# The MLP's first layer as seven block products with tokens on the partitions

## The chip, the core and the metric

The kernel runs on one core of a Trainium2 chip. A core has a matrix engine (TensorE, PE in the profile; its weight loads are PEld), VectorE (DVE), ScalarE (ACT), GpSimd (POOL) and SyncE (SP), each of which works through its own instructions in order and waits for the others by semaphores. SP, ACT and POOL issue DMAs. The metric is the device time of one execution in microseconds (us), the median of several runs.

## The reference, cut to what matters

One layer of a decoder trunk on 512 tokens of 2048 features, in float32. The mixing part and a cross-attention to 256 memory tokens come first; the change touches the MLP, the last norm, and how the cross-attention's last projection hands its result on.

```
h = h + memory_cross_attention(rmsnorm(h, g_xattn), rmsnorm(mem, g_mem), xa_wq, xa_wkv, xa_wo)
hn = rmsnorm(h, g_mlp)                                  # h: 512 x 2048
h = h + square(relu(hn @ w_ff1)) @ w_ff2                # w_ff1: 2048 x 8192, w_ff2: 8192 x 2048
return rmsnorm(h, g_final)
```

## The kernel before

**Three matmuls for one.** Every operand is split into a high part, rounded to the fast matmul format, and a low part, the rest. A product is hi·hi + hi·lo + lo·hi: three matmuls of 128x512 (L349 to L351 in the helper `mm`; L1490 to L1492 in the second layer). The high part is made by a cast on ACT, the low part by a subtraction on DVE that waits for the cast.

**First layer** (`mlp`, L1269 to L1301). Features lie on the partitions and the 512 tokens on the columns. 64 tiles `f` of 128 hidden features, each 16 blocks of the inner dimension by three matmuls into one PSUM bank (`ft`). `Stream` loads the weights on SP's queue, splits them three units ahead (L356 on ACT, L357 on DVE). `evac1` (L1275 to L1279) does relu and the norm's factor on DVE, the square on ACT, and ACT sends the tile to DRAM (`d_u`). After tiles 7, 15, 23 and 31 `res_T` (L1303) transposes a quarter of the residual to token rows, 16 transposes into four banks, and puts it back into the same SBUF tiles (`rp`, shown as `d`).

**Second layer** (`Second`, L1315). Tokens on the partitions, and a block scheme: activation and weight are cut in halves, and seven products of sums of halves take the place of eight. A *chunk* (eight of them) is one such scheme over 1024 hidden features: seven *products* n = 0 to 6, each of four *steps* `kk`; a step uses one weight block of 128x1024, or a sum of such blocks, and has 12 matmuls. For n = 0, 3 and 5 the block is a plain load on SP's queue; for n = 1, 2, 4 and 6 it is added by an accumulating DMA, issued by POOL, onto the block of an earlier product (L1352), which must wait until that one's low part is made (L1362). So cast (L1357), low part, accumulating DMA, cast of the sum is a chain from product to product. `prep` writes the casts four steps ahead of the matmuls, the low parts three, the loads seven. `stat` and `stat_low` (L1387, L1392) split the activation sums, one product ahead. `use` (L1494) adds or subtracts the four finished banks into the residual on DVE. `ahead` starts all this under the last six tiles of the first layer.

**End** (`Final`, L1502). While the last product runs, tokens 0 to 255 are normed: squares with row sums on ACT, factor, scaling on DVE, transposes back to features, gain during the evacuation, and out by SP. Then tokens 256 to 383 and 384 to 511, the latter wholly after the last matmul.

**Order.** Nothing schedules: each engine runs its instructions as the Python code emits them. PSUM has eight banks: four `mm`, three `st`, one `o`.

Of the kernel before, what the change touches and what calls it, by code (L numbers as in the profile page):

```python
# [72 lines left out]
def _units(a):  # L73
# [49 lines left out]
    feat("f1", a["w_ff1"][0].reshape(KT, 128, DFF), DFF // 128)  # L123
# [8 lines left out]
class _Null:  # L132
# [8 lines left out]
    def __getitem__(self, k):  # L141
        return self
# [21 lines left out]
class Slots:  # L164


    def __init__(self, pool, name, n, cols):
        self.pool, self.name, self.cols = pool, name, cols
        self.free, self.of, self.low = deque(range(n)), {}, n

# [6 lines left out]

    def put(self, t):
        self.free.append(self.of.pop(id(t))[0])


class Stream:
# [4 lines left out]
    def __init__(self, k, dram, order, info):  # L187
# [5 lines left out]
        self.last = len([t for t in order if t[0] != "f2"]) if order else 0  # L193
# [116 lines left out]
class Layer:  # L310
    def __init__(self, tc, ctx, a, order, info):
# [16 lines left out]
        self.d_u = dr.tile([8, 2, 2, 128, 4, 256], F32, name="d_u")  # L328
        self.slots = Slots(sp, "s", N_SLOTS, 1024)
# [874 lines left out]
    def cross(self, rate):  # L1204
# [29 lines left out]
        self.HG = [self.slot_hl() for _ in range(KT)]  # L1234
        self.acc = self.PP[:, 2048:]
        later = deque()
        for f in range(4):
            ps = [self.new_mm() for _ in range(4)]
            for h in range(2):
                w = self.W.get(("xo", f, h))  # L1240
                for kk in range(2):
                    k = 2 * h + kk
                    if f == 0 and k == 3:
                        self.side.drain()
                    for j in range(4):
# [4 lines left out]
                        if later and k < 3:  # L1250
                            self.res_use(later.popleft(), G_MLP, self.HG, st)
# [6 lines left out]
        while later:  # L1258
            self.res_use(later.popleft(), G_MLP, self.HG, st)
        self.put(*self.pt, *ks, *vs, *sl, *ssl, *self.oX)  # L1260

    def res_use(self, d, g, hg, st):
        self.split(hg[d], self.RES[d], self.gains[:, g + d:g + d + 1])
# [3 lines left out]
    def mlp(self, out):  # L1267

        nc = self.nc  # L1269
        tmp, sl = self.halves(2)  # L1270
        us, usl = self.halves(4)

        def evac1(f, ps):
            t, u = tmp[f % 2], us[f % 4]
            nc.vector.scalar_tensor_tensor(t, ps, 0.0, self.rbc, op0=OP.max, op1=OP.mult)  # L1275
            nc.scalar.activation(u, t, AF.Square)  # L1276
            c, h, k = f // 8, f // 4 % 2, f % 4
            nc.scalar.dma_start(self.d_u[c, h, :, :, k, :].rearrange("t p n -> p t n"),
                                u.rearrange("p (t n) -> p t n", t=2))  # L1279

        def on1(k):
            if k == 1:
                self.rx3 = self.col_stats(self.acc, "rx3")
            if k == 6:
                self.bcast(self.rx3, self.rbc)

        ps0 = self.ft("f1", 0, self.HG)
# [334 lines left out]
```

## Time and profile before

| | us |
|---|---|
| median of 3 runs (2961.63 to 2963.34) | 2962.59 |
| the profiled execution | 2963.05 |
| its span in the trace | 2961.0 |
| PE busy / DVE / ACT / POOL | 2909.2 / 1648.9 / 1237.9 / 295.4 |
| first layer: 1603.4 to 2310.1 | 706.7 |
| second layer up to the last product: 2310.1 to 2919.4 | 609.3 |
| last product, last norm and output: 2919.4 to the end | 41.6 |

The engines' busy times overlap, so they don't add up to the span. [...] DVE and ACT rows follow each other closer than their durations too.

### The profile page before, as it was taken

How to read it: one execution, taken by the hardware profiler on the slowest of the kernel's cores; microseconds unless marked ns; L12 is line 12 of the kernel's file. 1: busy time of each engine (PE TensorE's matmuls, PEld its weight loads, DVE VectorE, ACT ScalarE, POOL GpSimd, SP SyncE). 2: the span in 40 equal slices, each digit the busy share in tenths (PEclk: the TensorE clock that was granted, in tenths of full speed). 3: DMA queues.
4: the chain of work that ended last, by engine and by line, in shares of the span. 5: the costliest groups of instructions: out<-in, count | busy, mean ns of one | idle time of the engine just before them, and what ended most of it. 6: DMA issues, size and time to landing. Idle time of an engine off the chain costs nothing.

```text
span 2961.0 us, 38469 instructions
## 1 busy us (share of the span) xinstructions
PE 2909.2 (98%) x14386; PEld 2483.1 (84%) x14386; DVE 1648.9 (56%) x3112; ACT 1237.9 (42%) x2460; POOL 295.4 (10%) x524
## 2 busy tenths in 40 slices
PE   8999999999999999999999999999999999999997
PEld 8999989888888888888887888888888788888885
DVE  6346666655555555554457332322333688888886
ACT  6345555544444444323345322322222444444444
POOL 3110200011001001001103000000000111111110
PEclk9999999999999999999999999999999999999998
DMA  4321212222233346543322334333335788888884
GB/s 154 105 71 57 66 54 65 62 93 93 93 100 97 121 132 201 172 140 119 118 84 89 118 118 121 118 117 121 125 119 166 183 218 218 218 222 217 216 220 123
DMA packets 139067, 387.85 MB, mean 131 GB/s; under 512 B 14208, under 2 KB 37120, under 8 KB 138880
## 3 DMA queue, kind: packets, MB, share of 16 engines
q1 hardware_dynamic: 96128, 288.92, 30.6%
q0 software_dynamic: 18432, 67.12, 11.8%
q10 hardware_dynamic: 24320, 29.37, 2.8%
q8 instruction: 112, 1.84, 0.3%
q14 instruction: 75, 0.61, 0.1%
HBM read 351.79 MB, written 33.55 MB: 130 GB/s over the span
## 4 chain that ended last, share of the span: by engine, by line
PE 88%; DVE 4%; ACT 3%; issue 3%; DMA 2%; POOL 0%; SPq 0%; ACTq 0%; POOLq 0%; DVEq 0%
PE mm L349 21%; PE mm L351 21%; PE mm L350 21%; PE mm L1492 3%; PE mm L1490 3%; PE mm L1491 3%; PE st L570 2%; PE st L1492 2%; PE st L1491 2%; PE st L1490 2%; DMA s<-wts 2%; DVE s L357 1%; PE o L587 1%; PE o L588 1%; PE st L351 1%
## 5 line engine op out<-in xcount | busy, mean ns | idle before, releaser
L349 PE MATMUL mm<-s,s 128*128 128x512 f32 (+5 forms) x3032 | 1152.3, 380 | 7.2 <-ACT s L356 5.4
L351 PE MATMUL mm<-s,s 128*128 128x512 f32 (+5 forms) x3032 | 1128.1, 372 | 2.8 <-DVE s L360 2.8
L350 PE MATMUL mm<-s,s 128*128 128x512 f32 (+5 forms) x3032 | 1127.2, 372 | 0.2 <-DVE s L357 0.2
L357 DVE TENSOR_TENSOR s<-s,s 128x512 fp32r<-128x512 f32 (+4 forms) x814 | 533.8, 683 | 445.9 <-ACT s L356 442.4
L349 PEld LDWEIGHTS mm<-s,s 128*128 128x128 f32 x3032 | 572.1, 189 | 96.5 <-issue 8.0
L351 PEld LDWEIGHTS mm<-s,s 128*128 128x128 f32 x3032 | 570.7, 188 | 92.7 <-DVE s L360 4.8
L350 PEld LDWEIGHTS mm<-s,s 128*128 128x128 f32 x3032 | 572.5, 189 | 81.6 <-DVE s L357 1.3
L356 ACT CAST s<-s 128x512 fp32r<-128x512 f32 (+4 forms) x814 | 451.7, 586 | 313.4 <-PE mm L350 156.7
L1357 ACT CAST s<-s 128x1024 fp32r<-128x1024 f32 x224 | 227.3, 1049 | 273.2 <-DMA s<-wts 262.9
L1362 DVE TENSOR_TENSOR s<-s,s 128x1024 fp32r<-128x1024 f32 x224 | 269.9, 1222 | 77.1 <-ACT s L1357 76.0
L497 ACT ACTIVATE PP<-PP,mx 128x512 f32<-128x512 f32 (+1 forms) x208 | 116.3, 559 | 274.6 <-DVE mx L496 273.9
L1352 POOL DMA_DIRECT2D s<-wts x128 | 111.5, 871 | 1179.2 <-DVE s L1362 1037.7
L357 DVE TENSOR_TENSOR s<-st,s 128x512 fp32r<-128x512 f32 (+5 forms) x265 | 140.6, 540 | 111.6 <-ACT s L356 110.6
L1492 PE MATMUL mm<-s,s 128*128 128x512 f32 x512 | 200.3, 391 | 1.7 <-DVE s L1392 1.4
L1491 PE MATMUL mm<-s,s 128*128 128x512 f32 x512 | 199.9, 390 | 1.7 <-DVE s L1362 1.7
L1490 PE MATMUL mm<-s,s 128*128 128x512 f32 x512 | 200.6, 392 | 0.0
L1275 DVE SCALAR_TENSOR_TENSOR s<-mm,rbc 128x512 f32<-128x512 f32 x64 | 44.3, 692 | 276.9 <-PE mm L351 276.9
L1276 ACT ACTIVATE s<-s 128x512 f32<-128x512 f32 x64 | 40.4, 632 | 365.3 <-DVE s L1275 365.3
L356 ACT CAST s<-st 128x512 fp32r<-128x512 f32 (+5 forms) x265 | 117.4, 458 | 49.0 <-PE st L447 29.3
L496 DVE CUSTOM_DVE_ANT_0 PP<-st,cst 128x512 f32<-128x512 f32 (+1 forms) x208 | 99.9, 481 | 45.9 <-PE st L351 45.2
L1492 PEld LDWEIGHTS mm<-s,s 128*128 128x128 f32 x512 | 96.4, 188 | 24.5 <-DVE s L1392 4.5
L1492 PE MATMUL st<-s,s 128*128 128x512 f32 x288 | 112.6, 391 | 3.3 <-DVE s L1392 3.3
(235 smaller groups left out, 3076.7 us busy)
## 6 DMA issues: line engine op xcount, KB each, us to landing
s<-wts SPq DMA_DIRECT2D x388, 512.0 KB, 3.6
s<-wts POOLq DMA_DIRECT2D x128, 512.0 KB, 9.3
s<-wts SPq DMA_DIRECT2D x64, 352.0 KB, 3.0
d_u<-s ACTq DMA_DIRECT2D x64, 256.0 KB, 2.1
s<-d_u SPq DMA_DIRECT2D x32, 512.0 KB, 7.8
d_g<-s ACTq DMA_DIRECT2D x32, 256.0 KB, 2.0
s<-d_g SPq DMA_DIRECT2D x32, 256.0 KB, 4.0
s<-wts SPq DMA_DIRECT2D x16, 384.0 KB, 3.1
```

The lines of the kernel that those rows point to most:

```text
L349: t.matmul(ps, a.hr, b.hr, start=first, stop=False)
L350: t.matmul(ps, a.hr, b.lr, start=False, stop=False)
L351: t.matmul(ps, a.lr, b.hr, start=False, stop=last)
L356: nc.scalar.copy(o.hr, src)
L357: nc.vector.tensor_sub(o.lr, src, o.hi)
L497: nc.scalar.activation(p, p, AF.Exp, bias=mx, scale=-1.0, accum_out=sm)
L1352: self.nc.gpsimd.dma_start(t, src, accum_op=OP.add)
L1357: self.nc.scalar.copy(t.hr, self.raw[i])
L1362: self.nc.vector.tensor_sub(t.lr, r, t.hi)
L1490: m(ps, a.hr, b.hr, start=first, stop=False, skip_group_check=True)
L1491: m(ps, a.hr, b.lr, start=False, stop=False, skip_group_check=True)
L1492: m(ps, a.lr, b.hr, start=False, stop=last, skip_group_check=True)
```

## The change

**First layer in the second layer's manner.** `Mlp` takes the place of `mlp` and `Second`. Each of eight chunks now gives 1024 hidden features for all tokens in seven products over the 2048 inner features: 56 products, again of four steps of 12 matmuls, and then the 56 of the second layer, in one loop. The weight blocks (`f1` repacked on the host) use the same loads, accumulating DMAs, casts and low parts. The activation sums are formed in the first chunk and kept; `stat` splits two halves for each product. `use1` evacuates two banks after every product: copies on ACT for n = 0 to 2, add or subtract, relu and factor on DVE and squares on ACT for n = 3 to 6.

**Turned by transposes.** The result has tokens on the partitions, and the second layer needs features there. `u_T` does it: four transposes into the one `o` bank, a copy on ACT, a DMA to `d_u` issued by ACT; four such jobs after n = 4 and four after n = 6, one at the head of a step.

**Residual through DRAM.** `res_T` becomes 16 jobs in the first 16 steps, each four transposes into `o`, a copy on ACT and a DMA to `d_r`. Its SBUF is lent to weight blocks. Near the end of the first layer `res_in` reads it back, eight DMAs of 512 KB.

**Hand-over.** `res_use` writes the scaled input with two 256-column activations on ACT instead of a 512-column split. The first layer's first loads and splits run in the last quarter of the cross-attention's output projection (`f` = 3).

**End.** `gain_rows` spreads the last gain over the partitions by 16 small matmuls. `square` takes the row sums and multiplies the gain in before the factor is known, for all rows that are complete; the scaling is shared by DVE and ACT, and outputs leave by SP and ACT.

```
-    feat("f1", a["w_ff1"][0].reshape(KT, 128, DFF), DFF // 128)
+    f1 = a["w_ff1"][0].reshape(2, 4, 2, 128, 8, 2, 512)
...
+                        if f == 3 and j == 3:
+                            mlp.ahead(k)
...
-    def res_use(self, d, g, hg, st):
-        self.split(hg[d], self.RES[d], self.gains[:, g + d:g + d + 1])
+    def res_use(self, d, mlp, st):
+        for t in range(2):
+            self.nc.scalar.activation(mlp.x(d, t), self.RES[d][:, 256 * t:256 * t + 256], AF.Copy,
+                                      scale=self.gains[:, G_MLP + d:G_MLP + d + 1])
...
+        last = 2 * self.NP - 1
+        for p in range(last):
+            n, layer = p % 7, p // self.NP
...
+            for j in range(4):
+                i = 4 * p + j
+                self.prep(i + AHEAD)
+                if j == 0:
+                    self.blocks(p + 1)
+                if j % 2 == 0 and j // 2 < nh:
+                    self.stat(p + 1, j // 2)
+                if j % 2 and j // 2 < nh:
+                    self.stat_low(p + 1, j // 2)
+                for _ in range(1 + layer):
+                    if self.jobs and self.jobs[0][0] <= i:
+                        self.jobs.popleft()[1]()
+                self.part(p, j, ps, range(2))
...
+            (self.use2 if layer else self.use1)(p, ps)
+            if p == self.NP - 4:
+                self.res_in()
...
+    def use1(self, p, ps):
...
+            if n < 3:
+                nc.scalar.copy(o, ps[t])
+                continue
...
+            nc.vector.tensor_scalar(o, ps[t] if n == 6 else o, 0.0, r, op0=OP.max, op1=OP.mult)
+            nc.scalar.activation(o, o, AF.Square)
+        if n in (4, 6):
+            b = blk[1] if n == 4 else 0
+            cs = [C.pop((t, b)) for t in range(2)]
+            for j in range(4):
+                self.jobs.append((4 * p + 6, lambda j=j: self.u_T(c, b, j, cs, p == self.NP - 1)))
...
+    def u_T(self, c, b, j, cs, last):
+        k, nc = self.k, self.nc
+        ps, u = k.new_st() if last else k.new_o(), self.half()
+        for t in range(4):
+            o = t % 2 * 512 + j * 128
+            nc.tensor.transpose(ps[:, t * 128:t * 128 + 128], cs[t // 2][:, o:o + 128], k.ident)
+        nc.scalar.copy(u, ps)
+        nc.scalar.dma_start(k.d_u[c, b, :, :, j, :].rearrange("t p n -> p t n"), u.rearrange("p (t n) -> p t n", t=2))
...
+        self.gain_rows(Y)
+        self.prep(4 * p + 3)
+        for t in (0, 1, 2, 3):
+            for q in range(2, 4) if t > 1 else range(4):
+                self.square(t, q)
+        self.scale([0, 1])
+        for j in range(4):
+            self.part(p, j, X, [0])
+        self.use2(p, X, [0])
...
+        for t in range(2):
+            for q in range(4):
+                self.back(t, q, Y[q])
+        self.scale([2])
+        for j in range(4):
+            self.part(p, j, X, [1])
...
+    def square(self, t, q):
+        x = self.row(t, q)
+        self.nc.scalar.activation(self.sq[:, q % 2 * 512:q % 2 * 512 + 512], x, AF.Square,
+                                  accum_out=self.cols[:, 4 * t + q:4 * t + q + 1])
+        self.nc.vector.tensor_mul(x, x, self.g[q // 2][:, q % 2 * 512:q % 2 * 512 + 512])
```

**What stands on ACT in the first layer.** `s` are SBUF tiles, `PP` and `d` SBUF lent or shared, `o` the single PSUM bank. Before, inside the first layer (weight casts of 512 columns, a square and its store for each tile):

```order
L356 CAST s6_93<-s0_87 128x512 x2
L356 CAST s2_89<-s1_88 128x512 x2
L1276 ACTIVATE s11_14117<-s9_14115 128x512
L1278 DMA d_u_86<-s11_14117 128x2x256
L356 CAST s4_91<-s0_87 128x512 x2
L356 CAST s6_93<-s1_88 128x512 x2
```

In the changed kernel, from the third step of a product n = 5 to the second step of n = 6 (L1350 casts a weight block, L1423 an activation sum, L1540 squares, L1578 copies the transposed tile out of `o`, L1579 stores it):

```order
L1350 CAST s37_15345<-d0_10557 128x1024
L1423 CAST s9_15350<-s20_13692 128x1024
L1578 COPY s29_14128<-o_15353 128x512
L1579 DMA d_u_86<-s29_14128 128x2x256
L1350 CAST s21_15372<-PP_100 128x1024
L1578 COPY s15_14129<-o_15378 128x512
L1579 DMA d_u_86<-s15_14129 128x2x256
L1540 ACTIVATE d4_10556<-d4_10556 128x512 x2
L1350 CAST s24_15403<-d3_10555 128x1024
L1423 CAST s16_15408<-s12_13685 128x1024
L1578 COPY s15_14129<-o_15411 128x512
L1579 DMA d_u_86<-s15_14129 128x2x256
```

Each copy that frees the `o` bank now stands behind the casts of weights four steps ahead, and, at a product's start, behind the squares of the product just finished.

**What stands on ACT at the hand-over.** Before, the last four feature tiles (L359 split, L420 square for the norm) and then the weight casts of the first layer:

```order
L359 ACTIVATE s32_13699<-d0_10556,gains_95 128x512
L420 ACTIVATE s36_13683<-d0_10556 128x512
L356 CAST s2_89<-s0_87 128x512 x2
L356 CAST s4_91<-s1_88 128x512 x2
L356 CAST s6_93<-s0_87 128x512
```

In the changed kernel, after the last four feature tiles (the first cast, L1350, takes the first accumulated block; L1567 copies a residual tile out of `o`):

```order
L1350 CAST s17_14132<-PP_100 128x1024
L1423 CAST s33_14140<-s31_14137 128x1024
L1567 COPY s29_14128<-o_14143 128x512
L1568 DMA d_r_87<-s29_14128 128x512
L1350 CAST s39_14162<-PP_100 128x1024
L1567 COPY s15_14129<-o_14168 128x512
L1568 DMA d_r_87<-s15_14129 128x512
```

The first copy out of `o` (tile o_14143, which PE fills at the head of the layer's first step) now stands behind the cast of the first accumulated block.

**What stands on DVE at the end.** Before, from the last additions into the residual (L1497) to the factor of tokens 0 to 255 (L392 to L397):

```order
L1497 TENSOR_TENSOR d2_10553<-st_22613,d2_10553 128x512
L1497 TENSOR_TENSOR d3_10554<-st_22614,d3_10554 128x512
L1497 TENSOR_TENSOR d2_10553<-st_22615,d2_10553 128x512
L1497 TENSOR_TENSOR d3_10554<-o_22616,d3_10554 128x512
L1362 TENSOR_TENSOR s8_22671<-s35_22133,s19_22670 128x1024
L1521 TENSOR_REDUCE PP_99<-PP_99 128x2
```

In the changed kernel, from the last of these additions (L1553):

```order
L1553 TENSOR_TENSOR s27_18978<-o_23593,s27_18978 128x512
L1355 TENSOR_TENSOR s38_23648<-d4_10556,s12_23647 128x1024
L1641 TENSOR_TENSOR d4_10556<-d4_10556,d2_10554 128x512 x2
L1641 TENSOR_TENSOR s31_18977<-s31_18977,d0_10557 128x512 x2
L1641 TENSOR_TENSOR s27_18978<-s27_18978,d2_10554 128x512 x2
L1641 TENSOR_TENSOR s26_18979<-s26_18979,d0_10557 128x512 x2
L1641 TENSOR_TENSOR s37_18981<-s37_18981,d0_10557 128x512 x2
L1641 TENSOR_TENSOR s34_18983<-s34_18983,d0_10557 128x512 x2
L1647 TENSOR_REDUCE PP_100<-PP_100 128x2
```

Twelve multiplications by the gain (L1641), each behind its square on ACT, moved ahead of the first factor.

## Rows read from the trace of the kernel before

**Rows 1.** The page's part 1: busy us, share of the span, instructions.

```profile
PE 2909.2 (98%) x14386; PEld 2483.1 (84%) x14386; DVE 1648.9 (56%) x3112; ACT 1237.9 (42%) x2460; POOL 295.4 (10%) x524
```

**Rows 2.** Stretches: start:end, length, busy by engine, TensorE clock, DMA share, GB/s.

```profile
1603.40:2310.10 706.70, 705.40 (x3153) 585.37 (x3153) 217.86 (x330) 200.14 (x344) 6.18 (x4) 1.00 0.40 124
2310.10:2339.10 29.00, 24.02 (x97) 19.00 (x96) 19.99 (x20) 12.93 (x13) 7.09 (x8) 0.94 0.96 208
2339.10:2919.40 580.30, 578.64 (x2545) 476.98 (x2544) 477.50 (x511) 265.93 (x269) 104.38 (x120) 1.00 0.86 214
2919.40:2961.00 41.60, 21.39 (x113) 17.19 (x111) 22.30 (x65) 19.54 (x57) 0.00 (x0) 0.81 0.34 101
```

**Rows 3.** Timeline of PE (start, us, instruction): 40 matmuls apart; four transposes between matmuls.

```profile
2313.95 0.40 PE L1492 MATMUL mm<-s,s 128*128 128x512 f32 x1
...
2323.03 0.39 PE L1490 MATMUL st<-s,s 128*128 128x512 f32 x1
...
2932.39 0.60 PE L1542 MATMUL st<-cst,d 128*128 128x128 f32 x4
...
2932.75 0.48 PE L1490 MATMUL mm<-s,s 128*128 128x512 f32 x1
...
2933.06 0.39 PE L1491 MATMUL mm<-s,s 128*128 128x512 f32 x1
```

**Rows 4.** Timeline of PE at the second layer's start; in brackets idle time and releaser.

```profile
2312.21 0.50 PE L1491 MATMUL mm<-s,s 128*128 128x512 f32 x1 [1.69 <-DVE s L1362]
...
2326.94 0.50 PE L1492 MATMUL st<-s,s 128*128 128x512 f32 x1 [3.29 <-DVE s L1392]
...
2327.64 0.63 PE L1491 MATMUL st<-s,s 128*128 128x512 f32 x1
...
2330.91 0.40 PE L1490 MATMUL st<-s,s 128*128 128x512 f32 x1
```

**Rows 5.** Timeline of ACT in the first layer: square, store, next cast.

```profile
1807.01 0.63 ACT L1276 ACTIVATE s<-s 128x512 f32<-128x512 f32 x1 [5.77 <-DVE s L1275]
1807.67 0.37 ACTq L1278 DMA_DIRECT2D d_u<-s  x1
1808.13 1.66 ACT L356 CAST s<-s 128x512 fp32r<-128x512 f32 x3 [0.49 <-ACT s L1276]
```

**Rows 6.** The page's part 5: busy, mean ns of one, idle before and releaser.

```profile
L1357 ACT CAST s<-s 128x1024 fp32r<-128x1024 f32 x224 | 227.3, 1049 | 273.2 <-DMA s<-wts 262.9
L1362 DVE TENSOR_TENSOR s<-s,s 128x1024 fp32r<-128x1024 f32 x224 | 269.9, 1222 | 77.1 <-ACT s L1357 76.0
```

**Rows 7.** The accumulating DMAs of line L1352, issue to landing.

```profile
DMA to landing us min/median/max: 5.3/9.3/12.3
```

**Rows 8.** The page's part 6: issues, KB each, median us to landing.

```profile
s<-d_u SPq DMA_DIRECT2D x32, 512.0 KB, 7.8
```

**Rows 9.** Timeline of DVE, ACT and POOL at the hand-over to the first layer.

```profile
1591.47 2.47 DVE L1254 TENSOR_TENSOR d<-mm,d 128x512 f32<-128x512 f32 x4
...
1595.08 0.62 ACT L420 ACTIVATE s<-d 128x512 f32<-128x512 f32 x1
...
1606.01 6.41 POOL L421 TENSOR_TENSOR PP<-PP,s 128x512 f32<-128x512 f32 x4 [3.78 <-ACT s L420]
```

**Rows 10.** Timeline at the end: squares, reduce, scaling, last matmul, last gain.

```profile
2919.04 0.64 ACT L1517 ACTIVATE PP<-d 128x512 f32<-128x512 f32 x1
...
2919.80 0.64 ACT L1517 ACTIVATE PP<-d 128x512 f32<-128x512 f32 x1
...
2924.34 0.16 DVE L1521 TENSOR_REDUCE PP<-PP 128x2 f32<-128x8 f32 x1 [2.91 <-ACT PP L1517]
...
2925.76 3.26 DVE L1527 TENSOR_SCALAR d<-d,rx 128x512 f32<-128x512 f32 x8
...
2941.76 0.39 PE L1492 MATMUL mm<-s,s 128*128 128x512 f32 x1
...
2956.98 0.37 ACT L1550 ACTIVATE s<-o,gains 128x128 f32<-128x128 f32 x1 [0.42 <-DVE s L1552]
```

More of the change, by code (lines that the diff above doesn't have):

```diff
@@ L192, in __init__ @@
         self.log = []
-        self.last = len([t for t in order if t[0] != "f2"]) if order else 0
+        self.last = len([t for t in order if t[0] not in ("f1", "f2")]) if order else 0
     def src(self, tag):
@@ L1468, in run @@
-        fin = Final(k, out)
-        self.prep(4 * last + 3)
-        fin.stats([0, 1])
-        first = fin.steps([0, 1], Y)
-        for t in range(2):
-            for j in range(2):
-                for kk in range(4):
-                    self.mm(ps[2 * t + j], A, kk, t, self.hl[4 * last + kk], j, False, kk == 3)
-                    if t or j:
-                        next(first, None)
-                self.use(ps[2 * t + j], a, b, t, j, sign)
-            if t == 0:
-                fin.stats([2])
@@ new lines, in run, with part @@
+            (self.use2 if layer else self.use1)(p, ps)
+            if p == self.NP - 4:
+                self.res_in()
+        self.end(last, X, Y, out)
+    def part(self, p, j, ps, ts):
+        n = p % 7
+        B = self.hl[4 * p + j]
+        first, last = self.FIRST[n] and j == 0, j == 3
+        for t in ts:
+            if p < self.NP:
+                S = self.S[p, j // 2][0]
+                for i in range(2):
+                    o = (2 * j + i) % 4 * 256 + 128 * t
+                    self.mm(ps[t], S[:, o:o + 128], B[:, 512 * i:512 * i + 512], first and i == 0, last and i == 1)
+            else:
+                S, o = self.S[p, 0][0], 256 * j + 128 * t
+                for i in range(2):
+                    self.mm(ps[2 * t + i], S[:, o:o + 128], B[:, 512 * i:512 * i + 512], first, last)
+        if 1 in ts:
+            self.k.put(B.hi, B.lo)
+            if j == 3 or j == 1 and p < self.NP:
+                self.k.put(S.hi, S.lo)
@@ L1489, in mm @@
+    def mm(self, ps, a, b, first, last):
         m = self.nc.tensor.matmul
@@ new lines, in row, with end @@
+    def row(self, t, q):
+        return self.R[t][q // 2][:, q % 2 * 512:q % 2 * 512 + 512]
+    def end(self, p, X, Y, out):
+        k = self.k
+        self.out = out
+        k.put(*self.usl)
+        self.sq = k.slots.plain()
+        self.cols = k.acc
+        self.gain_rows(Y)
[7 more added lines that the diff above has]
+        self.use2(p, X, [0])
+        self.square(2, 0)
+        self.square(2, 1)
+        for t in range(2):
+            for q in range(4):
+                self.back(t, q, Y[q])
+        self.scale([2])
+        for j in range(4):
+            self.part(p, j, X, [1])
+        self.use2(p, X, [1])
+        self.square(3, 0)
+        self.square(3, 1)
+        for q in range(4):
+            self.back(2, q, Y[q])
+        self.scale([3])
+        for q in range(4):
+            self.back(3, q, X[q])
```

383 lines of the change are left out of this document (198 added, 185 removed).

## The prediction

> **What bounds the kernel.** I read the busy line first: PE 98% [rows 1], so a term counts only where it adds or takes PE time. Then the stretches [rows 2]. The first layer, 706.7 us, is PE throughout, with DVE and ACT under a third busy and the DMA at 0.40. The second layer between its start and its last product is PE too, but with DVE at 82%, ACT at 46% and the DMA at 0.86: that is the surrounding into which the first layer now moves. Two stretches are not PE-bound: the second layer's first 29.0 us and the last 41.6 us. Last I read pitches: 40 matmuls take 2323.03 - 2313.95 = 9.08 us, 0.227 us each [rows 3]. A step of 12 is 2.72 us, a product of 48 is 10.9 us.
>
> **1. Matmuls.** The first layer has 64 x 16 x 3 = 3072 matmuls, afterwards 56 x 48 = 2688. 384 fewer x 0.227 = -87.1 us, all of it on PE's path.
>
> **2. Transposes.** 64 jobs `u_T` of four. A group between matmuls costs 2933.06 - 2932.39 less one pitch, 0.44 us [rows 3]: +28.2 us. The residual's 64 transposes are there before and after. One spreading of the norm's factor over the partitions (four small matmuls, at that group's price twice) goes: -0.9 us.
> The row says that transposes are not paid at their duration: four take 0.60 us together. [...]
>
> **3. Start of the first layer.** The block scheme pays its start-up at the hand-over now. The old hand-over was nearly free: the first stretch has 1.3 us without PE [rows 2]. New chain: the first residual tile of `f` = 2 is ready at 1591.5 + 0.6 = 1592.1 [rows 9]; ACT then writes four tiles, about 1.27 us each (two half activations, estimated at 0.37 from a 512-column one at 0.62, and a square at 0.53), to 1597.3. A cast of the sum and one of the first block, 1.05 each [rows 6], to 1599.4; the low part, 1.22 [rows 6], to 1600.6; the accumulating DMA, 9.3 [rows 7], to 1609.9; its cast, and a cast of the next sum, to 1612.0; only then the copy that frees `o`, 0.6, at 1612.6. PE begins step 0 at 1603.4 and is at step 1's transposes at 1606.6: it waits 6.0 us. [...] POOL's four additions for the norm, 1.6 us each [rows 9], stand before the fourth accumulating DMA, so that it lands near 1623.7 and costs 1 us at product 1; the next ten steps each have a residual job and lose some 3 us in all in the way of term 4. Together 12 us against 1.3: +10.8 us (ends +5 and +18).
>
> **4. The `o` bank in every chunk.** One bank serves all jobs, so the transposes at the head of a step wait for the copy of the step before. That copy stands on ACT behind casts for four steps later. On ACT a job costs 0.59 for the copy and 0.45 until the next cast can start: from the end of the square at 1807.64 to the next cast is 0.49 us, since ACT waits to issue the store [rows 5]. I lay out one chunk with PE at 0.227, casts at 1.0 to 1.05, low parts at 1.22 [rows 6], accumulated blocks landing 9.3 after the low part [rows 7].
> - Product n = 6 begins at 0. ACT must first square the results of n = 5, which DVE finishes only at 1.25; squares end at 1.9. Two casts to 4.0, copy to 4.6. PE wants to transpose at 3.15: it waits 1.5 us.
> - n = 0 begins at 13.25 and its fourth block's low part is made at 15.3, behind the evacuation of n = 6. The sum for n = 1 lands at 24.65, its cast ends at 25.7, the copy behind it at 26.3. PE is there at 25.0: 1.35 us.
> - In n = 1 ACT copies two banks, casts a block and a sum, and copies at 30.45; PE is there at 29.5: 1.0 us.
> - n = 2 to 5 have no such wait in this layout, and low parts are ready 2 us or more before their step.
> 3.85 us a chunk; the first wait eight times, the others seven: 12.0 + 16.5 = +28.5 us. No row shows a short wait of this kind, hence both ends: nothing, since the second layer hardly waits for its weights after its start (2545 x 0.227 = 577.7 of 580.3 us [rows 2]), up to 50 us, if each of the 16 groups loses a whole queue of three casts, 3.1 us. I take the layout, which lies nearest to the durations of the rows.
>
> **5. Second layer.** Its start-up goes: 29.0 us for 96 matmuls, 21.8 us, is 7.2 us lost [rows 2, 4]. In one loop the weights are already running: -6.7 us with half a us left over. Reading back the residual puts 4.2 MB into a stretch where the DMA is 0.86 busy at 214 GB/s [rows 2], for which that rate needs 20 us; a 512 KB read takes 7.8 us there [rows 8]. Accumulated blocks in flight are held up, with 2 us or more of slack: +4 us, ends 0 and +13. The first layer's own DMA moves as much as the second's, at the same pace.
>
> **6. End.** Before: 22.4 us from 2919.4 to the last matmul, 19.2 from there to 2961.0 [rows 2, 10]. After, from the same zero: gain matmuls to 1.8 (16 x 0.11); four copies on ACT to 2.8; twelve squares at a pitch of 0.76 [rows 10], to 11.9, where eight were; the multiplications on DVE end at 12.6, the factor takes 1.42 (reduce to scaling [rows 10]), scaling starts at 14.05. PE has done half of the last product at 7.3 and waits until 14.5. Then 32 transposes; the second four groups need banks that DVE empties only after two additions and two multiplications, at 19.2. The second half of the product starts at 21.5, its last matmul at 26.8, later at the lower clock: 4.4 to 6.6 us late. Behind it, in place of 19.2: addition, square and product to 2.7, copies to 3.9, factor to 5.35, scaling, transposes and copies to 8.4, and 3.7 from the last evacuation to the end [rows 10]: 12.1, so 7.1 won. Net -1.5 us (ends -3 and +5).
>
> **Sum.** -87.1 + 28.2 - 0.9 + 10.8 + 28.5 - 6.7 + 4.0 - 1.5 = -24.7. The profiled execution took 2963.05 us, 2.05 more than its span, which stay. 2963.05 - 24.7 = 2938.3; it stands 0.46 above the median, so I say **2938 us**.
>
> **Rivals.**
> - **The `o` bank never stops PE.** If ACT keeps ahead, term 4 falls to nothing and term 3 to its lower end: 2938 - 28.5 - 5.8 = 2904; with a third of term 4 left, 2914. For it: after its start the second layer loses under 3 us to waits [rows 2]. Against: there no ACT instruction stood between two uses of a bank by PE within one step.
> - **Slower: accumulated blocks land later.** Each chunk has two links from low part to landing, n = 0 to 1 and 1 to 2, whose casts stand before copies that PE waits for. Every us over 9.3 then costs up to 2 us a chunk, 16 us in all. It decides from 1.5 us over, 10.8 us; the slowest landing now is 12.3 [rows 7], which as a median would add 48 us: 2986. Against: the DMA carries no more than in the second layer. 6%.
> - **Transposes at their full duration.** If the groups did not overlap here, each transpose would cost the last one's own 0.60 - 3 x 0.11 = 0.27 us [rows 3]: 256 x 0.16 = 41 us more, 2979. [...] Against: every group in the rows overlaps. 1%.
> - **Start-up and reading back at their upper ends**, +7 and +9, with the end at +5: 2938 + 22.5 = 2960.
> - **The matmuls are not saved.** In the built program's order PE has 3072 fewer of the first layer's matmuls and 2688 more of the second's kind, so this is out: 1%, the time would be 2938 + 87 = 3025.
>
> **Chances.** Forecast with its neighbourhood (2920 to 2950) 0.60; bank free (2900 to 2920) 0.20; upper ends (2950 to 2965) 0.12; later blocks 0.06; full transposes 0.01; matmuls not saved 0.01. The range reaches over the first two and half of the third: 2905 to 2957. A measurement of this kernel tells about 0.2%, 5.9 us, from no change. Faster by more: 0.60 + 0.20 + half of 0.12 and a little, 0.87; within: 0.06; slower: 0.07.
>
> **What would show it.** The first layer should take 683 to 690 us from the first product to the last, with PE's waits put down to ACT's copy out of `o`, some 1 to 1.5 us each, three in a chunk, and one of about 6 us in its first product. The second layer should start without a wait over 1 us. DVE in the first layer near 80% busy, DMA near 0.85. In the end PE should stand still for some 7 us in the middle of the last product, and 12 us should follow the last matmul. The forecast is wrong if PE in the first layer waits for low parts (blocks too late), if the waits at `o` are absent, or if the matmuls' pitch there is not 0.227.

## The result

| | us |
|---|---|
| median of 4 runs before | 2962.75 |
| median of 4 runs after (2923.53 to 2926.27) | 2925.05 |
| ratio after to before, 95% interval | 0.9873 (0.9856 to 0.989) |
| span of the profiled execution, before and after | 2961.0, 2923.1 |

The change wins 37.7 us; the forecast was 24.7 (2938, range 2905 to 2957). The sign and the range held, and the `o` bank does stop PE behind ACT's copies as forecast, but at one of the three places of the forecast's layout; at the layer's start the chain was another one, and several terms were off in size.

First the page's part 1 of the changed kernel (answers [rows 1]) and its stretches, as in [rows 2]: first layer from its first matmul to the second layer's first, second layer up to the last product, and the end.

```profile
PE 2857.5 (98%) x14282; PEld 2438.4 (83%) x14282; DVE 1896.4 (65%) x3224; ACT 1484.4 (51%) x2663; POOL 405.6 (14%) x652
```

```profile
1601.18:2283.14 681.96, 654.31 (x2999) 535.92 (x2998) 475.64 (x463) 438.70 (x535) 120.06 (x133) 0.99 0.85 212
2283.14:2883.36 600.22, 600.22 (x2658) 497.38 (x2656) 495.68 (x527) 277.36 (x281) 108.78 (x125) 1.00 0.88 218
2883.36:2923.10 39.74, 25.44 (x145) 22.34 (x143) 25.93 (x57) 22.64 (x55) 0.00 (x0) 0.89 0.39 106
```

Against [rows 2] the first layer is 24.7 us shorter, the second 9.1 (29.0 + 580.3 before), the end 1.9. The other 2.2 lie ahead of the first layer: its start was at 1600.3 to 1603.8 in the fourteen traces of this study, which have nearly all the work ahead of it in common, so that is scatter. In the first layer PE is busy 654 of 682 us; the second has no gap left. The waits of PE that remain (line that waits, tile, releaser, total us, times, longest), the five largest that stand on lines of the MLP:

```profile
PE o L1577 <- ACT s L1578: 12.5, 12, 1.4
PE o L1566 <- ACT s L1567: 8.7, 2, 7.3
PE o L1577 <- ACT d L1540: 6.4, 1, 6.4
PE st L1661 <- issue: 5.2, 1, 5.2
PE mm L1661 <- DVE s L1656: 3.5, 1, 3.5
```

L1577 is the transposes of `u_T`, L1566 those of `res_T`, L1661 those of the end.

To price terms I laid the trace out by steps: the time from the first matmul of a step to that of the next, less twelve pitches of 0.2268 us (a matmul shows a duration of 0.39 us there, but in a row the next one starts 0.227 us later). Over the 224 steps of the first layer this excess adds up to 72.3 us. "Loss" below is this excess without the transpose groups.

| term, us | forecast | measured |
|---|---|---|
| 1 matmuls | -87.1 | -87.1 (pitch unchanged) |
| 2 `u_T` groups, factor broadcast | +27.3 | +29.8 (64 x 0.48 - 0.9) |
| 3 start of the first layer | +10.8 | +9.4 (10.7 against 1.3) |
| 4 `o` bank in the chunks | +28.5 | +15.3 |
| 5 second layer's start; reading back | -6.7; +4 | -10.5; +9.3 |
| 6 end | -1.5 | -1.9 |
| ahead of the change | 0 | -2.2 |
| sum | -24.7 | -37.9 (as the spans) |

**Term 4 in the trace.** Timeline of the changed kernel at the head of a product n = 6 that begins at 1851.9 (start, us, instruction, in brackets idle time and releaser); first ACT, then the transposes on PE in front of the product's second step:

```profile
1852.99 0.63 ACT L1540 ACTIVATE d<-d 128x512 f32<-128x512 f32 x1 [0.73 <-DVE d L1539]
1853.53 1.03 ACT L1350 CAST s<-PP 128x1024 fp32r<-128x1024 f32 x1
1854.47 1.04 ACT L1423 CAST s<-s 128x1024 fp32r<-128x1024 f32 x1
1855.41 0.58 ACT L1578 COPY s<-o 128x512 f32<-128x512 f32 x1
```

```profile
1856.05 0.66 PE L1577 MATMUL o<-cst,s 128*128 128x128 f32 x4 [1.13 <-ACT s L1578]
```

Square of n = 5's result, two casts, copy: the order of the forecast, at 1.36 us in each of eight chunks by the step table (forecast 1.5). The other two waits of its layout, 1.35 and 1.0 us about the head of n = 1, are not there. In their place four of eight chunks lose 0.6 to 1.7 us in n = 5, which the layout had without a wait.

**Term 3 in the trace.** ACT, POOL and PE at the start of the changed kernel's first layer:

```profile
1606.18 0.63 ACT L442 ACTIVATE s<-d 128x512 f32<-128x512 f32 x1 [2.35 <-POOL PP L443]
...
1608.40 0.63 ACT L442 ACTIVATE s<-d 128x512 f32<-128x512 f32 x1 [0.78 <-POOL PP L443]
1608.93 1.03 ACT L1350 CAST s<-PP 128x1024 fp32r<-128x1024 f32 x1
...
1610.82 0.58 ACT L1567 COPY s<-o 128x512 f32<-128x512 f32 x1
```

```profile
1604.56 8.22 POOL L443 TENSOR_TENSOR PP<-PP,s 128x512 f32<-128x512 f32 x4
1612.73 0.89 POOL L1345 DMA_DIRECT2D s<-wts  x1
```

```profile
1611.44 1.12 PE L1566 MATMUL o<-cst,d 128*128 128x128 f32 x4 [7.27 <-ACT s L1567]
```

The copy ends at 1611.4 (forecast 1612.6) but not for the forecast's reason: the first accumulated block landed at 1603.2, 5.5 us after its issue. ACT reached its cast late because the squares (L442) waited for POOL's additions of the norm (L443), which took 2.05 us each, not 1.6 as in [rows 9].

**Term 5, reading back.** SP's queue, ACT and PE around the eight loads (L1587) of the residual:

```profile
2234.05 12.77 SPq L1587 DMA_DIRECT2D s<-d_r  x7
2249.32 0.33 SPq L1338 DMA_DIRECT2D s<-wts  x1
```

```profile
2259.35 1.04 ACT L1350 CAST s<-s 128x1024 fp32r<-128x1024 f32 x1 [10.79 <-DMA s<-wts]
2260.30 1.15 ACT L1540 ACTIVATE d<-d 128x512 f32<-128x512 f32 x2
```

```profile
2260.98 1.00 PE L1577 MATMUL o<-cst,d 128*128 128x128 f32 x2 [6.37 <-ACT d L1540]
```

The weight block of L1338 stands behind the loads, its cast on ACT waits for it, the squares stand behind the cast, and PE waits for the squares: 7.0 us, and 2.3 in the next step.

**Term 6.** PE in the last product: gain matmuls, the transposes of tokens 0 to 255, the last matmul:

```profile
2883.36 2.84 PE L1633 MATMUL st<-cst,gains 128*128 128x128 f32 x24
2886.03 1.06 PE L1633 MATMUL o<-cst,gains 128*128 128x128 f32 x8
...
2897.72 1.94 PE L1661 MATMUL st<-cst,d 128*128 128x128 f32 x8 [5.15 <-issue]
...
2909.35 0.40 PE L1518 MATMUL mm<-s,s 128*128 128x512 f32 x1
```

The last matmul starts 3.6 us later in the stretch than before (26.0 against 22.4; forecast 4.4 to 6.6), and 13.8 us follow it (19.2 before, 12.1 forecast). The 1.9 us that the stretch wins are no firm figure. Eight traces of this study have the same code at the end: in three of them, the changed kernel's among them, the stretch takes 39.3 to 39.8 us, and in five (e1, e2, e4, e5 and e11) 41.4 to 42.0, as long as the old end. In those five the mean granted clock of the stretch is 0.81 to 0.82 in place of 0.87 to 0.89. In the changed kernel the clock is 0.50 from 2897.7 to 2900.9, where transposes follow the stop of 5.15 us in the middle of the product, and 1.00 from 2902.3 to the last matmul.

### The profile page after: what moved, and what is told of

Read it like the earlier page. It is cut to its first block, busy times and chain, and to the rows that moved or that the text cites. A ratio compares the mean times of both kernels' runs of the same rounds, so it can differ in the third digit from the quotient of the medians.

```text
span 2923.1 us, 38769 instructions
## 1 busy us (share of the span) xinstructions
PE 2857.5 (98%) x14282; PEld 2438.4 (83%) x14282; DVE 1896.4 (65%) x3224; ACT 1484.4 (51%) x2663; POOL 405.6 (14%) x652
## 4 chain that ended last, share of the span: by engine, by line
PE 80%; issue 5%; DVE 4%; ACT 4%; DMA 4%; POOL 1%; SPq 0%; ACTq 0%; POOLq 0%; DVEq 0%
PE mm L371 13%; PE mm L373 13%; PE mm L372 13%; PE mm L1516 6%; PE mm L1518 6%; PE mm L1517 6%; PE st L1516 4%; PE st L1518 4%; PE st L1517 4%; PE st L592 2%; DMA d<-wts 2%; DVE s L379 1%; PE o L609 1%; PE o L610 1%; DMA PP<-wts 1%
## 5 line engine op out<-in xcount | busy, mean ns | idle before, releaser
L371 PE MATMUL mm<-s,s 128*128 128x512 f32 (+5 forms) x2008 | 752.7, 375 | 5.4 <-ACT s L378 5.2
L373 PE MATMUL mm<-s,s 128*128 128x512 f32 (+5 forms) x2008 | 729.5, 363 | 2.7 <-DVE s L382 2.6
L372 PE MATMUL mm<-s,s 128*128 128x512 f32 (+5 forms) x2008 | 728.6, 363 | 0.8 <-DVE s L379 0.8
L379 DVE TENSOR_TENSOR s<-s,s 128x512 fp32r<-128x512 f32 (+4 forms) x558 | 369.8, 683 | 240.0 <-ACT s L378 236.8
L371 PEld LDWEIGHTS mm<-s,s 128*128 128x128 f32 x2008 | 379.3, 189 | 54.3 <-issue 5.5
L373 PEld LDWEIGHTS mm<-s,s 128*128 128x128 f32 x2008 | 378.2, 188 | 52.6 <-DVE s L382 5.0
L372 PEld LDWEIGHTS mm<-s,s 128*128 128x128 f32 x2008 | 379.9, 189 | 42.3 <-DVE s L379 1.9
L1355 DVE TENSOR_TENSOR s<-d,s 128x1024 fp32r<-128x1024 f32 x262 | 317.6, 1222 | 145.5 <-ACT s L1350 141.4
L1516 PE MATMUL mm<-s,s 128*128 128x512 f32 x1024 | 403.4, 394 | 0.0
L1518 PE MATMUL mm<-s,s 128*128 128x512 f32 x1024 | 399.6, 390 | 0.0
L1517 PE MATMUL mm<-s,s 128*128 128x512 f32 x1024 | 399.2, 390 | 0.0
L378 ACT CAST s<-s 128x512 fp32r<-128x512 f32 (+4 forms) x558 | 305.3, 570 | 171.5 <-PE mm L372 54.4
L1350 ACT CAST s<-d 128x1024 fp32r<-128x1024 f32 x262 | 271.1, 1049 | 226.2 <-DMA d<-wts 186.7
L1516 PE MATMUL st<-s,s 128*128 128x512 f32 x672 | 266.4, 397 | 0.0
L1518 PE MATMUL st<-s,s 128*128 128x512 f32 x672 | 262.9, 391 | 0.0
L1517 PE MATMUL st<-s,s 128*128 128x512 f32 x672 | 262.6, 391 | 0.0
L1345 POOL DMA_DIRECT2D d<-wts x160 | 139.3, 871 | 694.5 <-DVE s L1355 542.2
L1518 PEld LDWEIGHTS mm<-s,s 128*128 128x128 f32 x1024 | 192.5, 188 | 40.7
L1517 PEld LDWEIGHTS mm<-s,s 128*128 128x128 f32 x1024 | 192.8, 188 | 38.8
L1516 PEld LDWEIGHTS mm<-s,s 128*128 128x128 f32 x1024 | 192.7, 188 | 38.6
```

Source lines behind the costliest of these rows:

```text
L371: t.matmul(ps, a.hr, b.hr, start=first, stop=False)
L372: t.matmul(ps, a.hr, b.lr, start=False, stop=False)
L373: t.matmul(ps, a.lr, b.hr, start=False, stop=last)
L378: nc.scalar.copy(o.hr, src)
L379: nc.vector.tensor_sub(o.lr, src, o.hi)
L1345: self.nc.gpsimd.dma_start(t, src, accum_op=OP.add)
```

## The experiments

Ratios are to the kernel before, with 95% intervals; the changed kernel has 0.9873. "First layer" is the stretch of the run's trace, 681.96 us in the changed kernel.

**Three banks for the transposes (e1_banks).** X alternates between two pairs of `mm` banks, and the idle pair serves the jobs beside `o`:

```
+        r = self.nu % 3
+        return self.idle[r - 1] if r else self.k.new_o()
...
-        ps, u = k.new_o(), self.half()
+        ps, u = self.bank(), self.half()
```

> Three PSUM banks in turn for the transposes (`o` and the two `mm` banks that the chunk does not use) in place of the one `o`. In the trace of the changed kernel PE loses 10.7 us at the head of n = 6 (1.33 in each of eight chunks), 4.4 in n = 5, and 9 at the start of the first layer, all of it in front of a transpose. Theory: it waits there because the copy that frees the one bank stands on ACT behind casts; with three banks these waits go, 2925 - 22 = about 2903 us (2899 to 2908), and only the 7 us in the chunk of the residual's reading back stay. Rival: PE without these waits runs into weights that are not ready, since the DMA is 0.86 busy; then waits for low parts or casts take their place and the time stays above 2915.

2905.8 us, 0.9809 (0.9794 to 0.9823): 19 us less.

```profile
1602.70:2263.99 661.29, 650.41 (x3000) 536.19 (x2998) 475.33 (x463) 437.61 (x535) 120.49 (x133) 0.99 0.87 219
```

The first layer is 20.7 us shorter. All waits in n = 5 and n = 6 outside the chunk of the reading back are gone (15.3 us); the loss at the start falls from 10.7 to 5.4. PE did not run into late weights. So the cause of term 4 is shown: the single bank.

**Reading back spread (e2_spread).** One load behind each of eight products:

```
-            if p == self.NP - 4:
-                self.res_in()
+            if 0 <= p - self.NP + 9 < 8:
+                self.res_in(p - self.NP + 9)
```

> The residual's eight loads of 512 KB one after each product from the 48th on, in place of eight in a row behind the 53rd. In the trace of the changed kernel the block for the last step of n = 5 is issued on SP's queue at 2249.3, behind them, lands at 2259.3, ACT waits 10.8 us for it, and PE loses 9.3 us (7.0 and 2.3) in that chunk. Theory: the burst in front of one weight block is the price, spreading removes it: 2925 - 9 = 2916 us, no wait over 1.5 us in the last chunk of the first layer. Rival: it is the volume, 4.2 MB in a stretch whose DMA is 0.86 busy; then the loss is only spread, and the time stays at 2922 to 2926.

2919.9 us, 0.986 (0.9844 to 0.9877); the first layer is 672.63, 9.3 us shorter, and its last chunk loses no more than the others. (The time shows 5 of the 9: in this trace the first layer began 1.8 us later, and the end took 2.2 us more.) It was the burst in front of one weight block, not the volume.

**Residual jobs later (e4_late).**

```
-                self.jobs.append((0, lambda q=q, t=t: self.res_T(q, t)))
+                self.jobs.append((4, lambda q=q, t=t: self.res_T(q, t)))
```

> The 16 residual jobs begin in the fifth step of the first layer instead of the first; one bank as in the changed kernel. Theory: the 7.4 us wait in the second step, and about 1 us of lower clock behind it, is a wait for the copy out of the bank alone; the first accumulated block's low part is there at 1611.7 and PE needs it at 1612.1. So the wait goes: 2925 - 8 = 2917 us. Rival: the chain of the first accumulated blocks is late for PE anyway, and a wait of 5 us or more for a low part appears at product 1 instead: 2922 to 2926 us.

2928.7 us, 0.9887 (0.9872 to 0.9902): a miss. The wait in the second step went, and one of 7.12 us came in the sixth; the loss at the start is 12.9 instead of 10.7. POOL, ACT and PE of this run:

```profile
1605.13 8.32 POOL L443 TENSOR_TENSOR PP<-PP,s 128x512 f32<-128x512 f32 x4
1613.39 0.90 POOL L1345 DMA_DIRECT2D s<-wts  x1
```

```profile
1619.91 1.04 ACT L1350 CAST s<-s 128x1024 fp32r<-128x1024 f32 x1 [1.97 <-DMA s<-wts]
...
1624.43 0.58 ACT L1567 COPY s<-o 128x512 f32<-128x512 f32 x1
```

```profile
1625.06 1.11 PE L1566 MATMUL o<-cst,d 128*128 128x128 f32 x4 [7.12 <-ACT s L1567]
```

It is not a late low part, as the rival had it, but again the copy, now behind the cast of the fourth accumulated block, whose DMA POOL issued behind the four additions. While these blocks arrive, a copy stands behind one wherever the jobs begin.

**POOL's additions behind the fourth block (e10_adds).** The last four squares get own buffers, their additions stand behind the fourth accumulating DMA:

```
-        st, ssl = self.halves(2)
+        st, ssl = self.halves(4)
...
+                if p == 0 and j == 0:
+                    for x in self.adds:
+                        self.nc.gpsimd.tensor_add(k.acc, k.acc, x)
```

> At the hand-over the last four squares for the norm have four buffers instead of two, and POOL's four additions of them stand behind the fourth accumulating DMA; one bank, residual jobs from the first step. In the trace of the changed kernel the first accumulated block lands at 1603.2 (5.5 us after its issue), but ACT casts it at 1608.9, because two squares wait for POOL's additions (2.4 and 0.8 us); the fourth accumulating DMA is issued at 1612.7, behind these. Theory: POOL's additions hold the start; the cast moves to about 1606, the wait in front of the second step falls from 7.3 to 4 to 5 us, the fourth block lands at 1614 in place of 1618.9: 2925 - 4 = 2921 us. Rival, the one of the forecast: the accumulated block's landing holds it; then the wait stays at 7 us and the time at 2925.

2925.2 us, 0.9876 (0.9861 to 0.989): the step as expected, the gain not. Counted from the first matmul, the first block's cast came 3.3 us earlier, the wait was 4.1 us, the fourth block landed 6.7 us earlier. But 1.5 us of the gain went in the next step, where matmuls started every 0.43 us until 1615.9, and POOL's additions now stand in front of the next block:

```profile
1607.39 0.88 POOL L1351 DMA_DIRECT2D s<-wts  x1 [0.94 <-ACT s L1298]
1607.95 8.29 POOL L1485 TENSOR_TENSOR PP<-PP,s 128x512 f32<-128x512 f32 x4
1616.19 1.76 POOL L1351 DMA_DIRECT2D PP<-wts  x2
```

The fifth block's DMA went out at 1616.19, and the fifth to eighth steps lost 2.8 us more than in the changed kernel (11.8 us against 10.7 at the start in all). That POOL's additions, not the landing, held the first cast is shown; that they alone set the 10.7 us is not.

**Transposes doubled (e3_double), on the kernel with three banks.**

```
-        for t in range(4):
+        for t in (0, 1, 2, 3, 0, 1, 2, 3):
```

> The kernel with three banks (2905.8 us), but each of the 64 `u_T` groups transposes its four tiles twice into the same bank: 256 transposes more, the same copies and stores. Theory: a transpose costs its pitch, 0.11 us, so 256 x 0.11 = 28 us more, 2934 us. Rival one: it costs its duration beyond what overlaps, 0.27 us by the last one of a group: 69 us more, 2975. [...] Rival two: PE has time to spare in front of the groups and the price is partly hidden: under 15 us, 2920 or less.

2932.6 us, 0.9904 (0.9889 to 0.9919): 26.8 us more; first layer and the second's first steps are 27.8 us longer in the traces, 0.109 for each of 256. The first half of a doubled group on PE:

```profile
1703.89 0.38 PE L1586 MATMUL o<-cst,d 128*128 128x128 f32 x2
1704.11 0.38 PE L1586 MATMUL o<-cst,PP 128*128 128x128 f32 x2
```

A pair starts every 0.22 us while it shows 0.38 of duration. Both rivals fall; nothing of the price is hidden. One transpose shows 0.38 - 0.11 = 0.27 us in the trace, but that is not what one costs in a row.

**The four jobs after n = 4 three steps later (e5_shift).**

```
-                self.jobs.append((4 * p + 6, lambda ...
+                self.jobs.append((4 * p + (9 if n == 4 else 6), lambda ...
```

> The four transpose jobs after n = 4 three steps later: one in each of the last three steps of n = 6 and one in the first step of the next chunk, instead of the last two steps of n = 5 and the first two of n = 6. One bank as before. Theory: a wait arises where one job stands in the first step of a product and the next in the second, because ACT in between squares the finished products and casts; moved, 10.7 us in n = 6 and about 4 in n = 5 go: 2925 - 14 = 2911 us. Rival: the copy is always that late behind casts; then similar waits of 1 to 1.5 us appear at the new places and the time stays within 2922 to 2928.

2917.3 us, 0.9848 (0.9833 to 0.9862): 7.8 us less where 14 were expected, between the theory and its rival; the first layer is 671.17, 10.8 shorter. The 10.9 us at the head of n = 6 are gone with the one bank kept, so they come from two jobs about a product's head. Some 2.5 of n = 5's 4.4 us came back at the new places.

**The link that the layout had too long (e11_link).** POOL does two more additions between the low part of n = 0's fourth block and its accumulating DMA, in seven chunks, into an SBUF tile taken for them:

```
+            if n == 1 and j == 3 and not layer and c:
...
+                lo = self.hl[i - 4].lo[:, :512]
+                for h in range(2):
+                    self.nc.gpsimd.tensor_add(self.extra[:, 512 * h:512 * h + 512], lo, lo)
             self.nc.gpsimd.dma_start(t, src, accum_op=OP.add)
```

> The changed kernel with two extra additions on POOL, in chunks 1 to 7 of the first layer, between the low part of n = 0's fourth block and the accumulating DMA behind it. In the trace of the changed kernel this link takes about 6 us from low part to landing (in chunk 3 from 1866.8 to 1872.9), where the forecast put 9.3; with the additions, at 1.3 to 2.1 us each, it should be 9 to 10. Theory: the forecast's layout of a chunk was right and this one duration wrong, so at 9.3 its waits appear, 1.35 us before n = 1 and 1.0 in it: seven chunks of 2.35 = 16 us more, 2941 us. Rival: something else in the layout was wrong (casts, copies or where the jobs stand), and the chunk has the slack anyway: no wait over 0.3 us there and 2923 to 2927 us.

2938.0 us, 0.9921 (0.9905 to 0.9938): 13 us more; in the trace, whose execution is the slowest of the four (2942.2), the first layer is 697.24, 15.3 longer. The link from low part to landing went from 5.8 to 6.3 us in these chunks to 8.7 to 10.3. The waits of PE from 1700 to 2230, which is chunks 1 to 6 and the head of 7, in the changed kernel and here:

```profile
PE o L1577 <- ACT s L1578: 10.2, 10, 1.4
```

```profile
PE o L1583 <- ACT s L1584: 20.5, 24, 2.0
```

By the step table 15.0 of the 15.3 us lie in n = 0's last step and n = 1's first two: where the forecast put 2.35 us a chunk, and nearly in that size (2.1). In chunk 3 the cast waits 3.9 us for the landing, and the copy behind the cast frees the bank late, as the forecast had it. The additions also slow DVE's subtractions beside them, from 1.2 to 1.8 to 2.1 us, but DVE has 2.1 us to spare before the next one. About n = 1 the layout was right; one duration in it was not.

**The old end (e7_oldend).** `end` put back to the order of the kernel before, the rest as changed.

```
-        self.gain_rows(Y)
...
+        fin = Final(k, out, self.row)
+        fin.stats([0, 1])
+        first = fin.steps([0, 1], Y)
```

> The changed kernel with the end of the kernel before: no gain matmuls, the gain in the evacuation, four more squares behind the last matmul, output by SP alone, the last product by output tiles. Theory: the reordered end is worth the 1.9 us by which its stretch in the two traces differs (39.7 against 41.6), so 2927 us, with 22 us to the last matmul and 19 behind it. Rival: the old end is dearer or cheaper in this kernel, where the residual lies in other tiles: a stretch off by over 1.5 us from 41.6.

2927.5 us, 0.9882 (0.9866 to 0.9899). The last stretch is 40.9 us, 22.1 to the last matmul and 18.8 from there: 1.2 us more than in the changed kernel. That is less than the new end differs between traces of the same code (39.3 to 42.0), so no gain of the reordering is shown.

**The last gain by DMA (e8_gaindma).** A row of the gain is read to all partitions by two DMAs:

```
-        self.gain_rows(Y)
...
+            self.nc.sync.dma_start(self.g[b], bass.AP(tensor=g.tensor, offset=g.offset + 1024 * b, ap=[[0, 128], [1, 1024]]))
```

> The last gain comes to all partitions by two DMAs of a row of it, about two products before the end of the second layer's last chunk but one, in place of 16 gain matmuls and four copies in the last product. In the trace of the changed kernel these matmuls take 3.5 us on PE (32 records at 0.11, twice what was forecast), and ACT's squares begin 4.1 us after the last matmul before them. Theory: both PE's first half of the last product and the chain squares, factor, scaling begin 3.4 us earlier: 2921.6 us. Rival: the chain begins with the last additions into the residual on DVE, which do not move; then PE waits 3 us longer in the middle of the product and the time stays at 2924 to 2926.

2924.7 us with a scatter of 2920.2 to 2929.5, 0.9875 (0.986 to 0.989): the time tells nothing. In the trace the last stretch is 36.6 in place of 39.7 us, as expected, and the wait in the middle of the product did not grow by 3:

```profile
2892.73 0.69 PE L1657 MATMUL st<-cst,d 128*128 128x128 f32 x2 [5.52 <-DVE d L1652]
```

**Together.** e12_noadds has three banks, spread reading back and the gain by DMA; e9_all also POOL's additions behind the fourth block.

> Three banks, the spread reading back and the last gain by DMA together. Theory: the three act in different places (transposes' waits, one chunk's weight block, last product), so their gains add up: 2905.8, less 9.5 for the 7.6 and 1.9 us that the three-bank kernel loses in the last chunk, less 3.2 for the end: 2893 us. Rival: with PE faster the DMA, 0.86 busy, becomes late and takes back part: over 2898 us.

> The same three, and the last four squares at the hand-over with four buffers and POOL's additions of them behind the fourth accumulating DMA. Alone, with one bank, this moved a wait from the second step to later steps and won nothing. Theory: that was because the copies out of the one bank stand behind the next casts; with three banks the 4 to 5 us that PE still loses in the first two products get smaller: 2 us less than the kernel without it, 2891 us. Rival: ACT's work in these products sets the pace, and the two kernels are equal within 1 us.

2899.1 us, 0.9789 (0.9774 to 0.9803), and 2898.1, 0.9787 (0.9773 to 0.9802): equal within the scatter. Both are above the 2893 and 2891 expected. The first layer behaves (652.5 and 650.0 us), but in the second, which lost nothing before, some steps of the last two chunks lose 3 to 5 us in all, where ACT's casts wait for weight blocks behind the two gain DMAs. (In e8_gaindma the same two DMAs stand at the same place and its second layer lost 0.1 us there, so by themselves they cost nothing there.) The last kernel sets these apart (e13_best):

```
-            if p == last - 10:
-                self.gain_rows()
+            if p in (last - 14, last - 7):
+                self.gain_rows(p // (last - 7))
```

> The kernel with all four edits (2898.1 us), but the two DMAs of the last gain stand apart, one behind product n = 6 of the last chunk but one and one a chunk later, instead of both behind the same n = 3. In the trace of the kernel before it, PE loses 4.5 us in two steps of the last chunk but one of the second layer, where casts wait for weight blocks behind these two DMAs on SP's queue. Theory: as with the residual's reading back, a load alone costs nothing and two in a row in front of weight blocks do: the 4.5 us go, 2894 us. Rival: the second layer has no slack left for 1 MB more at a DMA share of 0.87, wherever it stands: 2897 to 2900 us.

2893.2 us (2891.5 to 2895.9), 0.9769 (0.9756 to 0.9782): 32 us less than the changed kernel, 69 less than the one before. Its three stretches:

```profile
1601.00:2251.00 650.00, 647.61 (x3000) 534.52 (x2998) 475.11 (x463) 438.44 (x535) 121.02 (x133) 1.00 0.88 221
2251.00:2854.00 603.00, 600.91 (x2655) 496.26 (x2654) 491.83 (x526) 279.50 (x282) 109.03 (x125) 1.00 0.89 220
2854.00:2891.00 37.00, 22.51 (x116) 19.24 (x114) 26.28 (x58) 19.94 (x51) 0.00 (x0) 0.84 0.41 114
```

PE is busy in all but 2.4 of the first layer's 650.0 us, at a DMA share of 0.88. The loss in the last two chunks is gone. The second layer is still 2.8 us longer than in the changed kernel (600.2): some 2.9 us are lost in its first two chunks, and why was not tried.

## Why the prediction was right, and where its sizes failed

**Term 4 carries the miss**, 13.2 us by itself; the other terms are off by up to 5.3 us each and cancel, which is luck. The step that failed is "accumulated blocks landing 9.3 after the low part": a median over all places of a product [rows 7], put on the one link on which the waits about n = 1 rest. In the second layer it fits that very link: its eight DMAs take 8.6 to 10.8 us in the trace before, 9.0 as the median. In the first layer the link takes 6 us, 5.7 of them the DMA. The queues in the two places, in the changed kernel, first layer (1867 to 1873) and then second (2440 to 2449), as shares of 16 engines:

```profile
q0 software_dynamic: 239, 0.84, 81.7%
```

```profile
q0 software_dynamic: 289, 1.05, 59.0%
q1 hardware_dynamic: 391, 1.41, 45.0%
```

q0 are the accumulating DMAs, q1 SP's loads. In the second layer SP loads weight blocks just then, and in the first it loads nothing: its queue stands still for 25.7 us (to 1880.3 in chunk 3) until a transpose of L1577 has read the result that still lies in the next block's SBUF tile. The second layer's first chunk bears the reading out: there SP loads nothing beside this DMA, and it takes 5.7 us, while in the seven chunks after it, with 1.4 to 1.5 MB of SP's loads beside it, it takes 8.7 to 9.6. The queues in that first chunk (2285.6 to 2291.3):

```profile
q0 software_dynamic: 251, 0.90, 92.5%
```

No run changed these loads, so this reason is read from traces, not tested. "At the same pace" was true of the layer's mean (0.85 against 0.88) and false of this place. e11_link makes the link as long as forecast and gets the forecast's waits. The 4.4 us in n = 5, where the layout had no wait, are waits for the copy out of the one bank too, since they go with three banks. What sets their size is open: the fourth plain block of n = 5 takes 14.5 to 16.7 us to land in chunks 1 to 6, and casts and copies stand behind it, but 1.7 us are lost where it took 15.3 and 0.1 where it took 15.1.

**Term 3** came out within 1.4 us by luck, from a wrong chain (and its 12 less 1.3 is 10.7, not 10.8). It took ACT to be ready and the landing late; the trace and e10_adds show the landing early and ACT held by POOL's additions. What it had right, the fourth accumulating DMA behind these additions, is what the expectation of e4_late left out. Of its 12 us, 2 stand for slower matmuls behind the wait, a size that no run shows: in the changed kernel PE lost some 1.4 us there, at a granted clock of 0.50 from 1611.4 to 1614.1, and in e10_adds, behind a wait of 4.1 us, the step's twelve matmuls took 5.3 us, 2.5 more than twelve pitches.

**Term 5** has two errors that nearly cancel. The second layer before lost 3.3 us after its start (580.3 - 2544 x 0.2268), which I let stand and which went too. The reading back was sized by volume and slack, +4, but its price is its place in one queue: 9.3, and nothing when spread.

**Terms 1, 2 and 6** held. A group is 0.48 us, not 0.44: the six pitches after the first matmul behind it are 0.228 to 0.236 us in place of 0.227, and the forecast's reading stopped before them. In the end the 16 gain matmuls are 32 records and 3.5 us, twice the forecast, and the squares begin only behind their copies; the shorter way behind the last matmul paid for it, though the stretch differs by 2 us between traces of the same code. The upper end of the 4.4 to 6.6 us reckoned with slower matmuls behind the stop, which the changed kernel does not show: the clock was 0.50 in transposes ahead of the product's second half, which itself ran at 1.00.

**The rivals.** The `o` bank does stop PE (15 us in the chunks), so the first one is out, though 13.2 of the 28.5 us that set it apart were not paid. Later blocks did not come; e11_link shows that rival's mechanism at one of its two links, but only one landing there came later than the forecast's 9.3 us (10.3), so its price is hardly tested. Of the things to be seen, DMA share, the second layer's start, a long wait in the first product (7.3 us for 6) and the stop in the middle of the last product (5.2 us for 7) were there, and the first layer came out just below its range (682.0 for 683 to 690). Three waits in a chunk were not there; DVE is at 70% in the first layer, not 80, since it evacuates two banks a product there and the second layer four.

## What to carry to other kernels

A duration for a link in a chain is read at that link, or at the place with the same neighbours in the queues, not from the median of its line. An end with a stop of PE in it is judged from several traces, since the same code took 39.3 to 42.0 us here, at a mean granted clock of 0.89 to 0.81. A read that is cheap by its volume was dear here in front of the one block that an in-order engine waited for (9.3 us, and nothing when spread): spread such loads, one at a time between the others. When a PSUM bank is freed by an engine that also does casts in order, look first for banks that lie idle in that stage.

## What was not expected of the hardware

POOL's additions and DVE's subtractions took longer where they ran side by side. Timeline of DVE at the start of the first layer in the changed kernel, while the four additions of term 3 run on POOL (1604.6 to 1612.8) and just after:

```profile
1604.22 3.02 DVE L1355 TENSOR_TENSOR s<-s,s 128x1024 fp32r<-128x1024 f32 x1
1607.17 2.28 DVE L1396 TENSOR_TENSOR s<-s,s 128x1024 f32<-128x1024 f32 x1
1609.99 1.66 DVE L1355 TENSOR_TENSOR s<-PP,s 128x1024 fp32r<-128x1024 f32 x1 [0.55 <-ACT s L1350]
1611.57 2.29 DVE L1428 TENSOR_TENSOR s<-s,s 128x1024 fp32r<-128x1024 f32 x1
1613.79 1.21 DVE L1355 TENSOR_TENSOR s<-PP,s 128x1024 fp32r<-128x1024 f32 x1
```

1.2 us each by themselves, 1.7 to 3.0 beside POOL, whose four additions took 8.22 us here and 5.40 a little earlier, where DVE read one input from PSUM or stood still. In e11_link subtractions beside the extra additions took 1.8 to 2.1 us. Why was not tested.

A matmul of 128x128 with a broadcast gain column and the identity shows as two records of 0.11 us, a transpose of the same size as one. After the 7.27 us wait at the start PE lost some 1.4 us by stretched pitches until 1614.4, at a granted clock of 0.50, no more than after the 3.29 us wait in [rows 4], where eight matmuls took 2330.91 - 2327.64 = 3.27 us, 0.41 each. SP's queue needed 12.8 us to issue seven loads of 512 KB in a row. The first layer's start still loses some 3.6 us in e13_best; what they wait for was not tried.
